# Moving the sampled tokens' state space steps of a hybrid decoder layer, and gating them apart

## The chip, the core and the metric

The kernel runs on one core of a Trainium2 chip. Five engines work side by side, each through its own instructions in order: TensorE (PE, with its weight loads PEld) multiplies matrices from on-chip memory into accumulator banks, VectorE (DVE) and ScalarE (ACT) compute on tiles of 128 partitions and empty those banks, GpSimd (POOL) computes on tiles, and SyncE (SP) issues nearly all DMA transfers. The metric is the device time of one execution in microseconds.

## The reference

One layer of a recurrent decoder for two groups of requests: one prompt of 1024 new tokens with empty states, and 8 sampled tokens, each with its own saved states. In the kernel the two lie side by side as 1032 columns.

```
h = rmsnorm(x);  q, f, i, g, z, xbc, dt = split(h @ w_in)
group A: 8 heads of a gated linear recurrence on q, f, i, own rmsnorm, times silu(g)
group B: xs, B, C = silu(conv4(xbc));  per head of 64 (16 heads, 2 groups of B and C):
         S = exp(A dt) S + dt x B^T ;  y = S C + D x
         y = rmsnorm over each half of y * silu(z)     (512 values a token)
x = x + concat(oA, y) @ w_out;  then a gated MLP with conv3, and a last rmsnorm
```

For the prompt group B is computed as a scan over chunks of 128 tokens. For a sampled token it is one step: scale the saved state (64 x 128 a head) by exp(A dt), add the outer product of dt x and B, store it as an output, multiply by C and sum. The change is about this step, "the step" below. The other outputs are the new states of both recurrences and of both convolutions.

## The kernel before, in words

*Projection jobs.* w_in is worked off in jobs of 128 output columns: x0 to x11 (convolution inputs of group B; x8 to x11 are B and C), z0 to z7, and f, q, v, sg for each of the 8 heads of group A. A job has three chunks of 344 tokens, each 24 matmuls (`in_job`, L290): 8 slices of the inner dimension, three products of split numbers (hh, hl are the high and low part of the normalised input, wh and wl of the weights). After each chunk `evict` empties the bank; `begin` runs at the job's start, and `load_ahead` (L217) has then just written the weight load of the job after it. The order of the jobs is x0 to x3, x9, x11, x4 to x7, z0 to z3, f0, q0, v0, sg0, z4 to z7, f1, q1, v1, sg1, then f, q, v, sg of heads 2 to 7.

*What runs beside them.* `drive` (L266) mixes a stream of other work into the jobs: it yields weights, and so many job matmuls are placed between its pieces. The first scan, `ssd(0)`, is mixed into the jobs from x9 to x7, the second, `ssd(1)`, into z0 to v0; sg0 and z4 to z7 run alone; head 0 of group A is mixed into f1 to sg1, head 1 into f2 to sg2, and so on. A scan's chunk is `ssd_front` (L530: csb is the decay matrix, xdt the scaled input, bg and xp transposes) and `ssd_back` (L563: yo from the state S, st the new state, yd the part within the chunk, sT at the end the state to be stored).

*Ticks.* Each call of `step` (L249) is a tick and one job matmul; a job and its end are 73 ticks. `after(n, work)` (L229) has a piece of work written n ticks later.

*Who sets the order.* Only TensorE's instructions run in the order in which they are written. Those of the other engines and of SyncE's queue are ordered by a planner when the kernel is built: it goes through the program with a model of the times and gives each engine what is ready and was written first. Once built, the order of each is fixed, and an instruction that waits holds up those behind it. `fetch` (L172) ties a load to the queue place of the weight load written last before it: it stands behind that one on SyncE, not ahead.

*Buffers.* Tiles are named by tags with a fixed number of buffers: "ld" has 2 (the states Sd of the step and Sh of the heads, 128 x 512), "d" has 4 (Bb and Cb of the step, vb of the heads), "z" has 4 (sz, the gate). Of accumulator banks the tag "nx" has one, for small products; `vd` at a head's start (L847), `od`, `odp` and `dms` in it, `ms` of the gate and others use it in turn.

*The step.* `ssm_decode(g, i)` (L628) does tile i (two heads of 64) of group g for the 8 tokens in two halves of 4: load B and C of the tokens to all partitions (Bb, Cb) and the state (Sd); scale Sd on ScalarE (L641, four activations); Bb times dt x on VectorE (L642); add (L643); store (L644); Sd times C on GpSimd (L645); sum on VectorE (L646). At the end L647 writes y into the last 8 columns of the tile Xg[g][i] (named xbc in the profile), beside the prompt's 1024. The four tiles of group 0 are written at the begin of x5, x7, z0 and z1, those of group 1 at the begin of z4 to z7.

*The gate.* A z job's `evict` (L672) multiplies Y, the tile with prompt and sampled columns, by silu(z) and collects the squares in gacc; `rstd` (L686) sums them over partitions with TensorE (ms), `rows` and `tail` (L703) scale the tile and store all 1032 columns into mix_d, from which the output projection reads.

Of the kernel before, what the change touches and what calls it, by code (L numbers as in the profile page):

```python
# [8 lines left out]
F32 = mybir.dt.float32  # L9
F32R = mybir.dt.float32r  # L10
U8 = mybir.dt.uint8
AF = mybir.ActivationFunctionType
ALU = mybir.AluOpType
# [3 lines left out]
P = 128  # L17
DM = 1024
T = 1024
ND = 8  # L20
NT = T + ND
CH = 344
NCH = 3
# [16 lines left out]
QW = NT // 4  # L40
# [10 lines left out]
def hybrid_layer(  # L51
# [9 lines left out]
    V, A, G, PE, SP = nc.vector, nc.scalar, nc.gpsimd, nc.tensor, nc.sync  # L61
# [5 lines left out]
    dram = ctx.enter_context(tc.tile_pool(name="dscr", bufs=1, space=DRAM))  # L67
# [3 lines left out]
    def nm(s):  # L71
        cnt[0] += 1
        return f"{s}_{cnt[0]}"
# [4 lines left out]
    const = part.enter_context(tc.tile_pool(name="const", bufs=1, side="right"))  # L78
    small = part.enter_context(tc.tile_pool(name="small", bufs=2, side="right"))
    tmp = part.enter_context(tc.tile_pool(name="tmp", bufs=1, side="right"))  # L80

    def tl(tag, name, dt=F32):
        w, n = TAGS[tag]
        return (work if tag in ("hT", "big", "e", "g") else tmp).tile([P, w], dt, tag=tag, bufs=n, name=nm(name))
# [4 lines left out]
    def bank(s, tag="mx"):  # L89
        return psmx.tile([P, 512], F32, tag=tag, bufs=NBANK[tag], name=nm(s))  # L90

    def mm(out, lhsT, rhs, start=True, stop=True):
        PE.matmul(out, lhsT, rhs, start=start, stop=stop)  # L93
# [55 lines left out]
    def col(name, i=0):  # L149
        c = vlay[name] + i  # L150
        return vcol[:, c:c + 1]
# [20 lines left out]
    def fetch(dst, src):  # L172

        with tc.issue_after(last_w[0].ins):
            SP.dma_start(dst, src)
# [53 lines left out]
    def after(n, work):  # L229

        later.append([n, work])
# [106 lines left out]
    Xg = [[None] * 4 for _ in range(2)]  # L338
    BT, CT, S = [None, None], [None, None], [None, None]
    last11 = const.tile([P, XT, 11], F32, name="last11")  # L340
    mix_d = dram.tile([16, P, NT], F32, name="mix_d")
# [13 lines left out]
    def xbc_evict(j, ext, c, cs, ps):  # L355
        e = min(cs.stop, T)
        A.copy(ext[:, 3 + cs.start:3 + e], ps[:, :e - cs.start])
        if c == 2:
            V.tensor_copy(ext[:, 3 + T:3 + T + 32].rearrange("p (b r) -> p b r", r=4)[:, :, 3:4],
                          ps[:, T - cs.start:].unsqueeze(2))  # L360
            V.tensor_copy(last11[:, j, :], ps[:, CH - 11:])

    def xbc_close(j, ext):
        G.tensor_copy(ext[:, 3 + T:3 + T + 32].rearrange("p (b r) -> p b r", r=4)[:, :, 0:3],
                      bufT[:, j, :].rearrange("p (b r) -> p b r", r=3))
        n = T + 32
        acc = tl("big", "xbc")
        conv_tail(acc, ext, 4, "cw", "cb", j, XT, n)
        A.activation(acc[:, :T], acc[:, :T], AF.Silu)
        A.activation(acc[:, T:NT], acc[:, T + 3:T + 32:4], AF.Silu)  # L370
        return acc

    def xbc_job(j, put):
        ext = []
        def begin():
            ext.append(xbc_open())
            if j in (5, 7):
                ssm_decode(0, (5, 7).index(j))

        in_job(f"x{j}", OFF_X + j * P, lambda c, cs, ps: xbc_evict(j, ext[0], c, cs, ps), begin=begin, end=lambda: put(xbc_close(j, ext[0])))  # L380

# [20 lines left out]
    ones = keep.tile([P, P], F32, name="ones")  # L402
# [24 lines left out]
    for c, cs in enumerate(chunks):  # L427
        ps = psmm.tile([P, 512], F32, tag="mm", name=nm("dt"))
# [9 lines left out]
    for i in range(9):  # L438
        n = P if i < 8 else ND
# [7 lines left out]
    d_bc = const.tile([P, 8], F32, name="d_bc")  # L447
# [61 lines left out]
    ddb = const.tile([P, 2, 8, ND], F32, name="ddb")  # L509
# [104 lines left out]
    def d4(t):  # L614
        return t.rearrange("p (b n) -> p b n", n=P)
# [12 lines left out]
    def ssm_decode(g, i):  # L628
        j = g * 4 + i
        xdd = small.tile([P, 2, ND], F32, tag="xdd", name=nm("xdd"))  # L630
        xdec = Xg[g][i][:, T:NT]
        V.tensor_tensor(xdd[:, 0, :], xdec, ddb[:, 0, j, :], op=ALU.mult)
        for b0 in (0, 4):
            bs = slice(b0, b0 + 4)
            Bb, Cb = tl("d", "Bb")[:, :512], tl("d", "Cb")[:, :512]
            for t_, r in ((Bb, 2 * g), (Cb, 2 * g + 1)):
                fetch(t_, bc_d[r, bs].rearrange("b n -> (b n)").unsqueeze(0).to_broadcast([P, 512]))
            Sd = tl("ld", "Sd")
            fetch(d4(Sd), state_ssm[0, bs, 2 * j:2 * j + 2].rearrange("b h p n -> (h p) b n"))
            for b in range(4):  # L640
                A.activation(d4(Sd)[:, b, :], d4(Sd)[:, b, :], AF.Copy, scale=ddb[:, 1, j, b0 + b:b0 + b + 1])  # L641
            V.tensor_tensor(d4(Bb), d4(Bb), cb(xdd[:, 0, bs]), op=ALU.mult)  # L642
            V.tensor_tensor(Sd, Sd, Bb, op=ALU.add)  # L643
            SP.dma_start(ssm_sample[0, bs, 2 * j:2 * j + 2].rearrange("b h p n -> (h p) b n"), d4(Sd))  # L644
            G.tensor_tensor(Cb, Sd, Cb, op=ALU.mult)  # L645
            V.tensor_reduce(xdd[:, 1, bs], d4(Cb), axis=mybir.AxisListType.X, op=ALU.add)  # L646
        V.scalar_tensor_tensor(xdec, xdec, d_bc[:, j:j + 1], xdd[:, 1, :], op0=ALU.mult, op1=ALU.add)  # L647

    def rstd_of(dst, tmp, ps, n):

        A.activation(dst, ps, AF.Abs_reciprocal_sqrt, bias=epsc, scale=1.0 / n)
        V.scalar_tensor_tensor(tmp, ps, n * EPS, dst, op0=ALU.add, op1=ALU.mult)
        V.scalar_tensor_tensor(tmp, tmp, -0.5 / n, dst, op0=ALU.mult, op1=ALU.mult)
        V.scalar_tensor_tensor(dst, tmp, 1.5, dst, op0=ALU.add, op1=ALU.mult)

    gr_d = dram.tile([2, 4, QW], F32, name="gr_d")

    def ssm_gate(g):
        acc = []

        def z_job(i):
            j = g * 4 + i

            def begin():
                if i == 0:
                    acc.append(tl("g", "gacc"))
                if g:
                    ssm_decode(1, i)
                elif i < 2:
                    ssm_decode(0, i + 2)  # L670

            def evict(c, cs, ps):  # L672
                Y = Xg[g][i][:, cs]
                sz = tl("z", "sz")[:, :CH]
                A.activation(sz, ps, AF.Silu)
                V.tensor_tensor(Y, Y, sz, op=ALU.mult)
                if i == 0:
                    A.activation(acc[0][:, cs], Y, AF.Square)
                else:
                    A.activation(sz, Y, AF.Square)  # L680
                    (V if g or i == 3 else G).tensor_tensor(acc[0][:, cs], acc[0][:, cs], sz, op=ALU.add)
                if i == 3 and c == NCH - 1:
                    after(36, rstd)
            in_job(f"z{j}", OFF_Z + j * P, evict, begin=begin)

        def rstd():  # L686
            ps = bank("ms", "nx")
            for q in range(4):
                mm(ps[32 * q:32 * q + 32, :QW], ones[:, 0:32], acc[0][:, q * QW:(q + 1) * QW])
            nt = tl("z", "nt")  # L690
            rstd_of(nt[:, :QW], tl("z", "nt")[:, :QW], ps[:, :QW], 512)
            SP.dma_start(gr_d[g], nt[::32, :QW])
            after(36, rows)

        def rows():
            fetch(acc[0][:, :NT], gr_d[g].rearrange("a t -> (a t)").unsqueeze(0).to_broadcast([P, NT]))
            after(20, lambda: spread(tail(), 6))

        def tail():
            for i in range(4):  # L700
                j = g * 4 + i
                Y = Xg[g][i][:, :NT]
                V.scalar_tensor_tensor(Y, Y, col("sn", j), acc[0][:, :NT], op0=ALU.mult, op1=ALU.mult)  # L703
                SP.dma_start(mix_d[8 + j], Y)
                yield

        for i in range(4):
            z_job(i)
# [110 lines left out]
    def head_in(h):  # L819
        t = {}  # L820

        def f_end():
            f, k = t["f"], tl("big" if h else "e", "k")
            A.activation(f[:, :NT], f[:, :NT], AF.Identity, bias=lbt2[:, 0, h:h + 1], scale=lbt2[:, 1, h:h + 1])
            V.tensor_scalar(k[:, :NT], f[:, :NT], -1.0, 1.0, op0=ALU.mult, op1=ALU.add)
            t["k"] = k

        for n, off, func in (("f", OFF_F, AF.Tanh), ("q", OFF_Q, AF.Silu), ("v", OFF_I, AF.Copy),
                             ("sg", OFF_G, AF.Silu)):
            def evict(c, cs, ps, n=n, func=func):  # L830
                A.activation(t[n][:, cs], ps, func, scale=0.5 if n == "f" else 1.0)

            def begin(n=n):
                t[n] = tl("e" if h == 0 and n == "f" else "big", n)

            if h == H - 1 and n == "sg":
                in_job_last(f"{n}{h}", off + h * P, evict, begin)
            else:
                in_job(f"{n}{h}", off + h * P, evict, begin, f_end if n == "f" else None)
        return t  # L840
# [539 lines left out]
    with tc.manual_schedule(engines={mybir.EngineType.PE}):  # L1380
# [56 lines left out]
        for r0 in range(0, FT - RND, RND):  # L1437
# [3 lines left out]
            for m in range(0, KT, 2):  # L1441
                wh, wl = wload(w_down[0, rows, m * P:(m + 2) * P], nk, 2 * P)
                for i in range(2):
# [3 lines left out]
                    for c, cs in enumerate(quarters):  # L1447
                        ps = down(lambda k: (wh[:, k, :], wl[:, k, :]), nk, slice(i * P, (i + 1) * P), acts, c)
# [14 lines left out]
    for c in (3, 0, 1, 2):  # L1463
        cs = quarters[c]
# [3 lines left out]
        for t0 in range(cs.start, cs.stop, P):  # L1468
            n = min(P, cs.stop - t0)
# [49 lines left out]
```

## Time and profile before

| | |
|---|---|
| median of 3 runs | 1765.24 us (1763.6 to 1767.99) |
| the profiled execution | 1764.89 us |
| its span, first to last instruction | 1763.2 us |
| TensorE busy | 1709.8 us, 97% |
| VectorE busy | 1097.8 us, 62% |
| ScalarE busy | 778.7 us, 44% |
| GpSimd busy | 478.8 us, 27% |
| mean granted TensorE clock | 0.995 |

The profile is of one execution. A row of the timeline gives start, length, engine, line of the kernel, operation, output and inputs, and in brackets the idle time of the engine just before, with what ended it. L93 is the helper that writes every matmul, so matmuls are told apart by their tiles. "mm" is a projection job. The granted clock is the share of full speed at which TensorE was allowed to run in a slice. A row of a group of instructions ends with count, busy time, mean length in ns, and the idle time before them with what ended it.

Where the parts lie in the span: the first scan from 107 to 213 us, the second to about 334, z4 to z7 from 343 to 389, the heads of group A from there to 890.

### The profile page before, as it was taken

What the parts mean: (1) busy time and instruction counts of PE and PEld (TensorE: products, weight loads), DVE (VectorE), ACT (ScalarE), POOL (GpSimd) and SP (SyncE); (2) the same over time, 40 slices, a digit from 0 to 9 for tenths busy, and PEclk for the clock granted to TensorE, in tenths of its full rate; (3) what the DMA queues carried; (4) which work ended last, traced back from release to release, by engine and by line L of the source; (5) the groups of instructions that cost most, each with busy time, mean ns of one, the idle gap of its engine ahead of it and who ended that gap; (6) DMA issues with size and microseconds to landing.
All of it is one profiled execution on the core that took longest, in us unless ns stands there. A gap on an engine that the chain in (4) does not pass through costs nothing. (4 is left out here: it accounts for less than half of the span.)

```text
span 1763.2 us, 38543 instructions
## 1 busy us (share of the span) xinstructions
PE 1709.8 (97%) x16115; PEld 1659.4 (94%) x16115; DVE 1097.8 (62%) x1978; ACT 778.7 (44%) x1422; POOL 478.8 (27%) x485
## 2 busy tenths in 40 slices
PE   7999899999999999999799999999999999999998
PEld 6998789899999999999799989999999999999997
DVE  6668966566554554566636687776667767445545
ACT  7577686444434344344423374343333434111114
POOL 2103231111110110111220355666666664000002
PEclk9999999999999999999999999999999999999999
DMA  5355644553232332234336832222222226422312
GB/s 166 65 148 149 173 120 143 167 169 120 83 93 57 98 87 72 77 110 144 114 115 210 250 123 73 73 85 82 88 73 73 79 82 214 153 83 78 98 61 97
DMA packets 250132, 200.23 MB, mean 114 GB/s; under 512 B 47252, under 2 KB 220870, under 8 KB 249942
## 3 DMA queue, kind: packets, MB, share of 16 engines
q1 hardware_dynamic: 249670, 197.68, 37.0%
q8 instruction: 126, 2.06, 0.5%
q14 instruction: 48, 0.39, 0.1%
q0 software_dynamic: 288, 0.10, 0.0%
HBM read 155.17 MB, written 46.95 MB: 115 GB/s over the span
## 5 line engine op out<-in xcount | busy, mean ns | idle before, releaser
L93 PE MATMUL mm<-hl,wh 128*128 128x344 f32 x1248 | 406.1, 326 | 0.0
L93 PE MATMUL mm<-hh,wh 128*128 128x344 f32 x1248 | 405.6, 326 | 0.0
L93 PE MATMUL mm<-hh,wl 128*128 128x344 f32 x1248 | 402.8, 323 | 0.8 <-issue 0.8
L93 PEld LDWEIGHTS mm<-hl,wh 128*128 128x128 f32 x1248 | 236.1, 189 | 4.8 <-issue 4.2
L93 PEld LDWEIGHTS mm<-hh,wh 128*128 128x128 f32 x1248 | 236.1, 189 | 4.2 <-issue 3.4
L93 PEld LDWEIGHTS mm<-hh,wl 128*128 128x128 f32 x1248 | 236.3, 189 | 1.4 <-issue 1.2
L190 ACT CAST wh<-ws 128x1024 fp32r<-128x1024 f32 x96 | 100.6, 1048 | 254.9 <-PE dn L93 134.9
L93 PE MATMUL ub<-uh,wh 128*128 128x258 f32 x704 | 199.5, 283 | 4.2 <-DVE fext L1332 2.7
L93 PE MATMUL ub<-uh,wl 128*128 128x258 f32 x704 | 198.7, 282 | 0.0
L93 PE MATMUL ub<-ul,wh 128*128 128x258 f32 x704 | 198.6, 282 | 0.0
L93 PE MATMUL dn<-ah,wh 128*128 128x256 f32 (+1 forms) x640 | 181.1, 283 | 2.0 <-DVE x L1449 2.0
L93 PE MATMUL dn<-al,wh 128*128 128x256 f32 (+1 forms) x640 | 180.6, 282 | 0.0
L93 PE MATMUL dn<-ah,wl 128*128 128x256 f32 (+1 forms) x640 | 180.1, 281 | 0.0
L192 DVE TENSOR_TENSOR wl<-ws,wh 128x1024 fp32r<-128x1024 f32 x88 | 108.8, 1236 | 78.5 <-ACT wh L190 77.7
L93 PE MATMUL ua<-uh,wh 128*128 128x258 f32 x528 | 149.3, 283 | 1.5 <-DVE val L1344 1.3
L93 PE MATMUL mm<-mh,wh 128*128 128x258 f32 x512 | 146.9, 287 | 3.0 <-ACT x L1077 1.8
L93 PE MATMUL ua<-ul,wh 128*128 128x258 f32 x528 | 149.1, 282 | 0.0
L93 PE MATMUL ua<-uh,wl 128*128 128x258 f32 x528 | 148.4, 281 | 0.0
L93 PE MATMUL mm<-ml,wh 128*128 128x258 f32 x512 | 145.4, 284 | 0.9 <-DVE ml L1037 0.9
L93 PE MATMUL mm<-mh,wl 128*128 128x258 f32 x512 | 145.2, 284 | 0.0
L93 PEld LDWEIGHTS ub<-uh,wh 128*128 128x128 f32 x704 | 133.0, 189 | 4.9 <-DVE fext L1332 2.9
L1282 DVE TENSOR_TENSOR wl<-wt,wh 128x512 fp32r<-128x512 f32 x88 | 89.1, 1031 | 73.8 <-ACT wh L1281 73.8
(353 smaller groups left out, 3981.9 us busy)
## 6 DMA issues: line engine op xcount, KB each, us to landing
ws<-in_w_in_dram SPq DMA_DIRECT2D x52, 512.0 KB
ws<-in_w_up_dram SPq DMA_DIRECT2D x44, 512.0 KB
ws<-in_w_out_dram SPq DMA_DIRECT2D x24, 512.0 KB
act_d<-val SPq DMA_DIRECT2D x22, 516.0 KB
al<-act_d SPq DMA_DIRECT2D x22, 516.0 KB
ws<-in_w_down_dram SPq DMA_DIRECT2D x22, 512.0 KB
ml<-mix_d SPq DMA_DIRECT2D x48, 172.0 KB
csb<-cs_d SPq DMA_DIRECT2D x32, 256.0 KB
```

Source lines behind the costliest of these rows:

```text
L93: PE.matmul(out, lhsT, rhs, start=start, stop=stop)
L190: A.copy(wh[:, :n], ws[:, :n])
L192: V.tensor_tensor(wl[:, :n], ws[:, :n], wh[:, :n].bitcast(F32), op=ALU.subtract)
L1282: V.tensor_tensor(lo[:, cs], sums[name], hi[:, cs].bitcast(F32), op=ALU.subtract)
```

## The change

The sampled columns of group B leave the tiles of the prompt. Their input goes into a small tile xdk (8 tiles x 8 tokens), their silu(z) into szd; the scan's tiles keep 1024 columns, and the prompt's gate works on these alone.

The step is taken apart. At its place it writes only dt x and the six loads (the state now ahead of B and C); 36 ticks later the first half up to the product with C, at 56 the second half, at 64 and 84 the sums. It is written elsewhere: group 0 at the begin of sg0, z4, z5 and z6, group 1 at the begin of v2, v3, v4 and v5.

The gate of the sampled columns is new: after the fourth tile of a group, 20 ticks later the product with szd, its squares and their sum over the tiles (`decode_gate`); 40 ticks later a matmul with ones into a bank "dgs" of tag "nx", the reciprocal root, the scaling, and one store of 4 x 128 x 8 values into mix_d (`decode_norm`).

```diff
+    xdk = const.tile([P, 8, ND], F32, name="xdk")
+    szd = const.tile([P, 8, ND], F32, name="szd")
...
-        A.activation(acc[:, T:NT], acc[:, T + 3:T + 32:4], AF.Silu)
+        A.activation(xdk[:, j, :] if j < 8 else acc[:, T:NT], acc[:, T + 3:T + 32:4], AF.Silu)
...
             ext.append(xbc_open())
-            if j in (5, 7):
-                ssm_decode(0, (5, 7).index(j))
...
-        xdec = Xg[g][i][:, T:NT]
+        xdec = xdk[:, j, :]
         V.tensor_tensor(xdd[:, 0, :], xdec, ddb[:, 0, j, :], op=ALU.mult)
+        got = []
         for b0 in (0, 4):
             bs = slice(b0, b0 + 4)
             Bb, Cb = tl("d", "Bb")[:, :512], tl("d", "Cb")[:, :512]
+            Sd = tl("ld", "Sd")
+            fetch(d4(Sd), state_ssm[0, bs, 2 * j:2 * j + 2].rearrange("b h p n -> (h p) b n"))
             for t_, r in ((Bb, 2 * g), (Cb, 2 * g + 1)):
                 fetch(t_, bc_d[r, bs].rearrange("b n -> (b n)").unsqueeze(0).to_broadcast([P, 512]))
-            Sd = tl("ld", "Sd")
-            fetch(d4(Sd), state_ssm[0, bs, 2 * j:2 * j + 2].rearrange("b h p n -> (h p) b n"))
+            got.append((bs, Bb, Cb, Sd))
+
+        def front(bs, Bb, Cb, Sd):
             for b in range(4):
...
             G.tensor_tensor(Cb, Sd, Cb, op=ALU.mult)
+
+        def back(bs, Bb, Cb, Sd):
             V.tensor_reduce(xdd[:, 1, bs], d4(Cb), axis=mybir.AxisListType.X, op=ALU.add)
-        V.scalar_tensor_tensor(xdec, xdec, d_bc[:, j:j + 1], xdd[:, 1, :], op0=ALU.mult, op1=ALU.add)
+        def end():
+            back(*got[1])
+            V.scalar_tensor_tensor(xdec, xdec, d_bc[:, j:j + 1], xdd[:, 1, :], op0=ALU.mult, op1=ALU.add)
+            if i == 3:
+                after(20, lambda: decode_gate(g))
+        after(36, lambda: front(*got[0]))
+        after(56, lambda: front(*got[1]))
+        after(64, lambda: back(*got[0]))
+        after(84, end)
+    def decode_gate(g):
+        js = slice(4 * g, 4 * g + 4)
+        dg = small.tile([P, 6, ND], F32, tag="dg", bufs=1, name=nm("dg"))
+        V.tensor_tensor(xdk[:, js, :], xdk[:, js, :], szd[:, js, :], op=ALU.mult)
+        V.tensor_tensor(dg[:, 0:4, :], xdk[:, js, :], xdk[:, js, :], op=ALU.mult)
+        V.tensor_reduce(dg[:, 4, :], dg[:, 0:4, :].rearrange("p j b -> p b j"), axis=mybir.AxisListType.X, op=ALU.add)
+        after(40, lambda: decode_norm(g, js, dg))
+    def decode_norm(g, js, dg):
+        ps = bank("dgs", "nx")
+        mm(ps[:, :ND], ones, dg[:, 4, :])
+        rstd_of(dg[:, 4, :], dg[:, 5, :], ps[:, :ND], 512)
+        for j in range(js.start, js.stop):
+            V.scalar_tensor_tensor(xdk[:, j, :], xdk[:, j, :], col("sn", j), dg[:, 4, :], op0=ALU.mult, op1=ALU.mult)
+        SP.dma_start(mix_d[8 + js.start:8 + js.stop, :, T:NT].rearrange("j p b -> p j b"), xdk[:, js, :])
...
-                if g:
-                    ssm_decode(1, i)
-                elif i < 2:
-                    ssm_decode(0, i + 2)
+                if g and i < 3:
+                    ssm_decode(0, i + 1)
...
+                if c == NCH - 1:
+                    G.tensor_copy(szd[:, j, :], sz[:, n:])
+                sz = sz[:, :n]
                 V.tensor_tensor(Y, Y, sz, op=ALU.mult)
...
-                V.scalar_tensor_tensor(Y, Y, col("sn", j), acc[0][:, :NT], op0=ALU.mult, op1=ALU.mult)
-                SP.dma_start(mix_d[8 + j], Y)
+                V.scalar_tensor_tensor(Y, Y, col("sn", j), acc[0][:, :T], op0=ALU.mult, op1=ALU.mult)
+                SP.dma_start(mix_d[8 + j][:, :T], Y)
...
             def begin(n=n):
+                if h == 0 and n == "sg":
+                    ssm_decode(0, 0)
+                elif 2 <= h <= 5 and n == "v":
+                    ssm_decode(1, h - 2)
```

More of the change, by code (lines that the diff above doesn't have):

```diff
@@ L635, in ssm_decode @@
             Bb, Cb = tl("d", "Bb")[:, :512], tl("d", "Cb")[:, :512]
+            Sd = tl("ld", "Sd")
+            fetch(d4(Sd), state_ssm[0, bs, 2 * j:2 * j + 2].rearrange("b h p n -> (h p) b n"))
             for t_, r in ((Bb, 2 * g), (Cb, 2 * g + 1)):
                 fetch(t_, bc_d[r, bs].rearrange("b n -> (b n)").unsqueeze(0).to_broadcast([P, 512]))
-            Sd = tl("ld", "Sd")
-            fetch(d4(Sd), state_ssm[0, bs, 2 * j:2 * j + 2].rearrange("b h p n -> (h p) b n"))
+            got.append((bs, Bb, Cb, Sd))
+        def front(bs, Bb, Cb, Sd):
             for b in range(4):
-                A.activation(d4(Sd)[:, b, :], d4(Sd)[:, b, :], AF.Copy, scale=ddb[:, 1, j, b0 + b:b0 + b + 1])
+                A.activation(d4(Sd)[:, b, :], d4(Sd)[:, b, :], AF.Copy, scale=ddb[:, 1, j, bs.start + b:bs.start + b + 1])
             V.tensor_tensor(d4(Bb), d4(Bb), cb(xdd[:, 0, bs]), op=ALU.mult)
@@ L654, in rstd_of @@
         V.scalar_tensor_tensor(dst, tmp, 1.5, dst, op0=ALU.add, op1=ALU.mult)
-    gr_d = dram.tile([2, 4, QW], F32, name="gr_d")
+    gr_d = dram.tile([2, 4, 256], F32, name="gr_d")
     def ssm_gate(g):
@@ L666, in begin @@
                     acc.append(tl("g", "gacc"))
-                if g:
-                    ssm_decode(1, i)
-                elif i < 2:
-                    ssm_decode(0, i + 2)
+                if g and i < 3:
+                    ssm_decode(0, i + 1)
             def evict(c, cs, ps):
+                cs = slice(cs.start, min(cs.stop, T))
+                n = cs.stop - cs.start
                 Y = Xg[g][i][:, cs]
@@ L688, in rstd @@
             for q in range(4):
-                mm(ps[32 * q:32 * q + 32, :QW], ones[:, 0:32], acc[0][:, q * QW:(q + 1) * QW])
+                mm(ps[32 * q:32 * q + 32, :256], ones[:, 0:32], acc[0][:, q * 256:(q + 1) * 256])
             nt = tl("z", "nt")
-            rstd_of(nt[:, :QW], tl("z", "nt")[:, :QW], ps[:, :QW], 512)
-            SP.dma_start(gr_d[g], nt[::32, :QW])
+            rstd_of(nt[:, :256], tl("z", "nt")[:, :256], ps[:, :256], 512)
+            SP.dma_start(gr_d[g], nt[::32, :256])
             after(36, rows)
         def rows():
-            fetch(acc[0][:, :NT], gr_d[g].rearrange("a t -> (a t)").unsqueeze(0).to_broadcast([P, NT]))
+            fetch(acc[0][:, :T], gr_d[g].rearrange("a t -> (a t)").unsqueeze(0).to_broadcast([P, T]))
             after(20, lambda: spread(tail(), 6))
@@ L701, in tail @@
                 j = g * 4 + i
-                Y = Xg[g][i][:, :NT]
-                V.scalar_tensor_tensor(Y, Y, col("sn", j), acc[0][:, :NT], op0=ALU.mult, op1=ALU.mult)
-                SP.dma_start(mix_d[8 + j], Y)
+                Y = Xg[g][i][:, :T]
+                V.scalar_tensor_tensor(Y, Y, col("sn", j), acc[0][:, :T], op0=ALU.mult, op1=ALU.mult)
+                SP.dma_start(mix_d[8 + j][:, :T], Y)
                 yield
```

## Prediction

> **What bounds the kernel now.** I read the page's first part, then a table of busy time by stage, the gaps of the TensorE timeline, and what the other engines waited for just ahead of each gap.
>
> ```profile
> PE 1709.8 (97%) x16115; PEld 1659.4 (94%) x16115; DVE 1097.8 (62%) x1978; ACT 778.7 (44%) x1422; POOL 478.8 (27%) x485
> ```
> ```profile
> 100.00:165.00 65.00, 65.00 (x451) 61.10 (x451) 53.38 (x76) 54.03 (x105) 15.31 (x20) 1.00 0.57 148
> 165.00:240.00 75.00, 66.93 (x439) 60.38 (x439) 61.02 (x103) 53.89 (x118) 21.11 (x18) 0.95 0.67 173
> ...
> 318.00:340.00 22.00, 19.12 (x119) 17.65 (x118) 15.82 (x28) 7.79 (x17) 3.67 (x3) 0.92 0.57 171
> 340.00:820.00 480.00, 477.69 (x6028) 460.84 (x6027) 256.96 (x483) 209.78 (x366) 44.73 (x34) 1.00 0.34 101
> ```
>
> TensorE is the bound: 1709.8 of 1763.2 us busy, in an order written by hand. A change that adds no matmuls worth naming can only move its idle time and its clock. The table (time, PE, PEld, DVE, ACT, POOL, granted clock, DMA share) shows where the change could reach: 165 to 240 us, the end of the first scan, loses 8.1 us and has a clock of 0.95; 318 to 340, the end of the second, loses 2.9 us at 0.92; 340 to 820, in which z4 to z7 and the heads run, loses 2.3 us in 480. The gaps one by one (start of the matmul, its length, in brackets the idle time before it and what ended it):
>
> ```profile
> 173.15 1.09 PE L93 MATMUL yd<-csb,xdt 128*64 128x128 f32 x16 [1.49 <-DVE xdt L557]
> 179.61 0.65 PE L555 MATMUL xp<-ident,xbc 128*128 128x128 f32 x4 [1.19 <-DVE ecs L577]
> 192.08 0.33 PE L548 MATMUL bg<-ident,xbc 128*128 128x128 f32 x1 [1.28 <-DVE S L583]
> 206.57 1.19 PE L93 MATMUL yo<-xbc,S 128*128 128x128 f32 x8 [2.00 <-DVE S L583]
> 227.64 0.33 PE L555 MATMUL xp<-ident,xbc 128*128 128x128 f32 x1 [1.96 <-ACT xbc L369]
> ...
> 329.83 0.66 PE L608 MATMUL sT<-ident,S 128*128 128x128 f32 x4 [2.54 <-DVE S L583]
> ```
> ```profile
> 170.00:180.00 10.00, 7.31 (x56) 6.11 (x55) 8.03 (x11) 7.67 (x19) 2.49 (x2) 1.00 0.62 167
> ...
> 200.00:210.00 10.00, 8.00 (x44) 6.24 (x46) 10.00 (x14) 5.78 (x15) 4.03 (x3) 0.88 0.43 98
> 210.00:220.00 10.00, 10.00 (x72) 9.77 (x69) 9.79 (x20) 4.51 (x10) 1.29 (x1) 0.95 0.72 185
> 220.00:230.00 10.00, 8.04 (x48) 7.78 (x47) 5.32 (x9) 9.24 (x18) 2.03 (x2) 0.90 0.90 222
> 230.00:240.00 10.00, 10.00 (x62) 9.22 (x62) 6.76 (x12) 9.94 (x23) 3.66 (x4) 0.93 0.37 105
> ...
> 330.00:340.00 10.00, 10.00 (x56) 10.00 (x56) 7.08 (x13) 4.60 (x9) 2.63 (x2) 0.83 0.50 140
> ```
>
> The gaps of 1.96 us and more are each followed by a spell of lower clock; those of 1.19 to 1.49 are not (1.00 from 170 to 180). A spell costs the clock missing in its slices: 10 x (0.12 + 0.05) = 1.7 us after 206.57, 10 x (0.10 + 0.07) = 1.7 after 227.64, 10 x 0.17 = 1.7 after 329.83. What VectorE did ahead of the gaps:
>
> ```profile
> 171.80 0.69 DVE L642 TENSOR_TENSOR Bb<-Bb,xdd 128x512 f32<-128x512 f32 x1 [2.83 <-DMA Bb<-bc_d]
> ...
> 188.03 0.69 DVE L646 TENSOR_REDUCE xdd<-Cb 128x4 f32<-128x512 f32 x1 [1.19 <-POOL Cb L645]
> 190.28 0.69 DVE L646 TENSOR_REDUCE xdd<-Cb 128x4 f32<-128x512 f32 x1 [1.56 <-POOL Cb L645]
> ...
> 326.25 0.69 DVE L642 TENSOR_TENSOR Bb<-Bb,xdd 128x512 f32<-128x512 f32 x1 [2.15 <-DMA Bb<-bc_d]
> 328.49 0.69 DVE L642 TENSOR_TENSOR Bb<-Bb,xdd 128x512 f32<-128x512 f32 x1 [0.94 <-DMA Bb<-bc_d]
> ```
>
> These are lines of the sampled tokens' step, and VectorE, which works in order, stands still in them with the scan's xdt and S queued behind. So the step is what stops the scan's matmuls at 173, 192 and 330 directly. The gaps at 180 and 207 follow while VectorE is full (10.00 of 10 from 200 to 210).
>
> **The change, part by part.** *The step leaves the first scan.* Four steps now run beside x4 to z1. Each is, by these rows, 8 x 0.39 = 3.1 us of ScalarE, 2 x (0.69 + 0.71 + 0.68) = 4.2 of VectorE, 2 x 1.34 = 2.7 of GpSimd, and on SyncE's queue six loads and two stores of 256 KB:
>
> ```profile
> L641 ACT ACTIVATE Sd<-Sd,ddb 128x128 f32<-128x128 f32 x64 | 20.5, 391 | 13.3 <-DMA Sd<-in_state_ssm_dram 13.2
> ...
> L645 POOL TENSOR_TENSOR Cb<-Sd,Cb 128x512 f32<-128x512 f32 x16 | 21.4, 1336 | 68.1 <-DVE Sd L643 57.9 <-DMA Sd<-in_state_ssm_dram 10.2
> L643 DVE TENSOR_TENSOR Sd<-Sd,Bb 128x512 f32<-128x512 f32 x16 | 11.3, 711 | 0.0
> L642 DVE TENSOR_TENSOR Bb<-Bb,xdd 128x512 f32<-128x512 f32 x16 | 11.0, 694 | 18.0 <-DMA Bb<-bc_d 18.0
> L646 DVE TENSOR_REDUCE xdd<-Cb 128x4 f32<-128x512 f32 x16 | 10.9, 683 | 14.3 <-POOL Cb L645 14.3
> ```
>
> With it go the waits above. I take all five gaps from 173 to 228 as gone: 1.49 + 1.19 + 1.28 + 2.00 + 1.96 = 7.9 us, and their two spells of low clock, 3.4. Ends: 11.3 us, and 1.49 + 1.28 = 2.8 if only the gaps go whose releaser stood directly behind a wait of the step. I take the first, because the stage before it (100 to 165) does the same convolutions and scan, with one step in it, without a single TensorE gap.
>
> *Where the first group's steps go.* They are written at the begin of sg0, z4, z5 and z6, with the work 36 ticks or more later. But what is written late is not run late:
>
> ```profile
> 347.22 0.44 ACT L675 ACTIVATE sz<-mm 128x344 f32<-128x344 f32 x1
> ```
> ```profile
> 298.41 0.38 SPq L189 DMA_DIRECT2D ws<-in_w_in_dram  x1
> ...
> 320.88 0.39 SPq L189 DMA_DIRECT2D ws<-in_w_in_dram  x1
> 321.31 0.58 SPq L175 DMA_DIRECT2D Bb<-bc_d  x1
> ```
>
> The step now written at z4 had its first VectorE work at 326.25, 21 us ahead of z4's first eviction, because its loads stand right behind the weight load of z5 (320.88) and the planner fills a free place with what its model has ready. After the change z4's step is that of the first group's second tile, behind the same weight load: the gap of 2.54 us at 329.83 and its 1.7 I leave as they are. sg0's step stands behind the weight load before, that of z4 (298.41), so it falls into 299 to 318, inside the second scan, which had no step there. Its price: 0 by the step written at x5, which cost no gap, up to 2.54 + 1.7 = 4.2 by the one at 326. Five steps fell into scans (four of them with gaps), for 11.3 + 4.2 = 15.5 us: 3.1 each, and I take that, +3.1. The steps of z5 and z6 replace those that ran there without a gap, with no scan beside them: 0, which z matmuls cover, and up to 4.2 each by the same row.
>
> *The second group beside v2 to v5.* The step moves behind the head's Sh tiles, which hold both "ld" buffers until the od matmuls, half-way through each head. There the stage's VectorE is busy 257 of 480 us and ScalarE 210 of 480, so 4.2 and 3.1 us a head are covered. Queued behind a late step are the next head's Sh loads and what VectorE does on them:
>
> ```profile
>   DMA Sh<-in_state_hgrn_dram: 16.7, 11
> ```
> ```profile
> 327.81 1.28 ACT L641 ACTIVATE Sd<-Sd,ddb 128x128 f32<-128x128 f32 x4 [7.35 <-DMA Sd<-in_state_ssm_dram]
> ```
>
> VectorE already waits for Sh 11 times, 1.5 us each, and the stage hides it: I take 0. Upper end: a wait of 7.35, less the 1.5 that is hidden, plus 1.7 of clock, 7.6 a head. The weight loads behind these loads on SyncE have room: the one at 320.88 is for z5, whose matmuls begin after z4's eviction at 347.
>
> *The gate of the sampled columns.* Eight copies on GpSimd and, for each group, two products, a reduction, three steps of the reciprocal root and four scalings of at most 128x32 on VectorE, some 2 us a group at 0.17 to 0.2 each; on ScalarE one 128x8 activation and up to two table loads; one small store. All of it lies beside matmuls of the stage above, cost 0 there. What is on TensorE's path: the new matmul "dgs" comes 20 + 40 + 84 = 144 ticks after the begin of z6 (and of v5), and a job and its end take 73 ticks. So it stands one matmul ahead of the end of z7 (and of sg5), and the next thing TensorE does is the transpose "vd" of head 0 (of head 5), into the same one-buffer bank "nx". It must wait until dgs has been read by ScalarE and VectorE. The nearest rows are the same operations on "dms":
>
> ```profile
> 440.33 0.29 PE L93 MATMUL dms<-od,ones 128*128 128x8 f32 x2
> ```
> ```profile
> 441.15 1.28 ACT L651 ACT_TABLE_LOAD   x1
> 442.45 0.27 ACT L651 ACTIVATE od<-dms,epsc 128x8 f32<-128x8 f32 x1
> ```
> ```profile
> 442.75 0.17 DVE L652 SCALAR_TENSOR_TENSOR od<-dms,od 128x8 f32<-128x8 f32 x1 [0.83 <-ACT od L651]
> ```
>
> With the table there: 0.27 + 0.17 after the matmul and some hand-over, less the last job matmul (65.0 / 451 = 0.14), so about 0.6 each, 1.2 in all; with the table load in the chain 442.92 - 440.33 = 2.6 plus 1.7 of clock, 4.3 each. I take the lower, as ScalarE has little to do between evictions at a job's end and a table load waits for no matmul. Here the next activation starts 0.02 us after the load's end. The Trainium skill ("ScalarE: Activation LUTs", What ACT_TABLE_LOAD costs) counts about 1.38 us of draining on top of the 1.28; the trace shows none of it, and by that rule the higher end would be 1.4 more each. The two dgs matmuls themselves: 2 x 0.29 = 0.6. The prompt's gate shrinks from 1032 to 1024 columns: nothing.
>
> *Sum:* -7.9 - 3.4 + 3.1 + 1.2 + 0.6 = -6.4 us against the profiled execution's 1764.9 (span 1763.2 and 1.7 around it), which gives 1758.5. The median of the runs, 1765.2, is 0.3 above it: 1758.8.
>
> **Rivals.**
> *A. All gaps of the scans go:* the staged step lands later in VectorE's order, and sg0's and z4's cost nothing, the gap at 330 included: -11.3 - 4.2 + 1.8 = -13.7, 1751. For: at sg0 and z4 no scan stands next to where the steps are written. Against: the 21 us of advance.
> *B. The step was not what limited the scan.* VectorE was busy 61 of 75 us there; the gaps at 180, 207 and 228 name ecs, S and ScalarE's Silu, none of them the step's. If they stay with their clock, -2.8 + 3.1 + 1.8 = +2.1, 1767. Against: the calm stage from 100 to 165.
> *C. Slower: Sh behind Sd.* In heads 1 to 4 VectorE is planned to take the next head's Sh when the model has it, but its load now waits for the step's store to release "ld". From a wait of 1.5 + 2.0 = 3.5 us on, a head loses 2.0 of TensorE and 1.7 of clock: 4 x 3.7 = 14.8, and -6.4 + 14.8 = +8.4, 1773.6. For: the 7.35 above. Against: no gap of note between 340 and 820 in spite of 16.7 us of such waits.
> *D. The clock does not come back with the gaps.* Then 3.4 stay, and a step in a scan costs (7.9 + 2.5) / 5 = 2.1: -7.9 + 2.1 + 1.8 = -4.0, 1761.2. Against: each gap of 1.96 to 2.54 us has its spell and no shorter one has. The Trainium skill ("TensorE: Matmul & The Clock Gate", Part 1: The HAM clock gate) lets the throttle return only after an idle window of about 3.4 us, which would speak for D; in this trace shorter gaps did it, so the row decides.
>
> **How the numbers follow.** The forecast 0.47 (its own range 1753 to 1763), A 0.13, B 0.19, C 0.16, D 0.05. A measurement of this kernel can tell about 0.3%, 5.3 us, from no change: below 1759.9 is faster, above 1770.5 slower. Faster: 0.30 of the forecast and A, 0.43. Slower: 0.15 of C and 0.04 of B, 0.19. The rest, 0.38, is the same. The range runs from A (1750) to 1771, which leaves out most of C.
>
> **What would show it.** Right: no VectorE wait for Bb or Cb between 165 and 240, no TensorE gap over 1 us there and a clock of 1.00; L642 still well ahead of z4, and a gap near the sT transposes; a TensorE wait at vd in heads 0 and 5 alone, near 0.6 us; no gaps in the second halves of heads 1 to 4. Wrong: gaps that keep their place in the first scan with no step near (B); waits for Sh over 3.5 us (C); new stalls of the scan between 299 and 318 above 4 us.

## The result, and the profile after

The changed kernel takes 1775.53 us in the median of 7 runs (1770.23 to 1781.17), the kernel before 1763.96 beside it (1760.81 to 1767.99): a ratio of 1.0068, with an interval of 1.0051 to 1.0086. It is slower by 12 us, where 6 us less were forecast. The profiled execution of it took 1778.31 us, with a span of 1776.5; it is 2.8 us above the median, so the prices read from its trace may add up to that much more than the medians show.

The table by stage of the changed kernel (time, TensorE, its weight loads, VectorE, ScalarE, GpSimd, granted clock, DMA share, GB/s):

```profile
165.00:240.00 75.00, 75.00 (x531) 69.40 (x532) 52.09 (x87) 56.43 (x108) 16.74 (x18) 1.00 0.34 94
305.00:328.00 23.00, 18.86 (x117) 17.41 (x116) 21.08 (x35) 10.01 (x25) 6.57 (x5) 0.93 0.71 193
380.00:390.00 10.00, 10.00 (x77) 9.16 (x81) 5.17 (x17) 4.66 (x7) 4.33 (x4) 0.83 0.41 107
440.00:720.00 280.00, 266.25 (x3472) 254.88 (x3470) 148.52 (x297) 119.13 (x214) 33.31 (x25) 0.97 0.37 109
```

The end of the first scan, which had 66.93 busy us of 75 and a clock of 0.95, is full at 1.00. The stage of the heads, in which TensorE stood idle for only 0.8 us before, is not. The same 280 us of the kernel before:

```profile
440.00:720.00 280.00, 279.16 (x3788) 267.69 (x3788) 143.36 (x276) 120.57 (x195) 26.02 (x20) 1.00 0.29 84
```

The changed kernel's gaps of over 1 us in TensorE's timeline, from the end of the second scan to head 5:

```profile
318.29 0.63 PE L609 MATMUL sT<-ident,S 128*128 128x128 f32 x4 [3.51 <-DVE S L584]
379.97 0.27 PE L886 MATMUL vd<-ident,v 128*8 128x128 f32 x1 [2.54 <-DVE dg L684]
467.14 0.75 PE L93 MATMUL a<-q,f 128*32 128x32 f32 x64 [2.33 <-DVE q L925]
535.50 0.75 PE L93 MATMUL a<-q,f 128*32 128x32 f32 x64 [2.81 <-DVE q L925]
601.85 0.75 PE L93 MATMUL a<-q,f 128*32 128x32 f32 x64 [2.15 <-DVE q L925]
667.20 0.97 PE L93 MATMUL a<-q,f 128*32 128x32 f32 x64 [1.39 <-DVE q L925]
711.69 0.36 PE L886 MATMUL vd<-ident,v 128*8 128x128 f32 x1 [2.54 <-DVE dg L684]
```

Four of the seven stand in the first halves of heads 1 to 4, where the prediction saw nothing, and where the code writes nothing of the step. To see what each place costs with its clock, I took from the traces, one execution of each kernel, the start of each projection job and subtracted. The table gives this for some jobs, in us against the kernel before; a step from one column to the next is what the stretch between them cost. The other rows are of the first experiments below, whose jobs are the same.

| kernel | x4 | v0 | z7 | v1 | v2 | v3 | v4 | v5 | q6 | sg7 |
|---|---|---|---|---|---|---|---|---|---|---|
| changed | -0.3 | -12.8 | -11.6 | -7.5 | -2.8 | +2.2 | +7.7 | +10.6 | +14.1 | +14.0 |
| loads tied | -1.1 | -13.6 | -12.3 | -8.3 | -8.2 | -8.1 | -8.1 | -7.9 | -5.0 | -5.1 |
| another bank for dgs | -0.4 | -12.9 | -12.2 | -12.9 | -8.9 | -4.1 | -1.4 | +2.8 | +3.8 | +3.7 |
| store on GpSimd's queue | -1.1 | -13.6 | -12.4 | -9.6 | -9.7 | -9.7 | -9.7 | -9.7 | -7.8 | -7.8 |
| tied, with the bank | -0.6 | -13.1 | -11.7 | -13.1 | -13.2 | -12.4 | -12.4 | -11.5 | -11.8 | -11.9 |

So the first scan gains 12.5 (x4 to v0) and the second's end loses 1.2 (v0 to z7); the gate at head 0 costs 4.1 (z7 to v1) and at head 5 3.5 (v5 to q6); between them four heads cost 4.7, 5.0, 5.5 and 2.9, 18.1 in all (v1 to v5). That makes +14.0 at sg7. The span's end is 13.3 later.

What VectorE does ahead of the gap at 467, in head 1 (L647 is the product of B, L642 in the kernel before and L649 where the loads are tied):

```profile
456.29 1.27 DVE L647 TENSOR_TENSOR Bb<-Bb,xdd 128x512 f32<-128x512 f32 x1 [1.61 <-DMA Bb<-bc_d]
464.18 0.69 DVE L647 TENSOR_TENSOR Bb<-Bb,xdd 128x512 f32<-128x512 f32 x1 [6.62 <-DMA Bb<-bc_d]
...
466.32 0.67 DVE L925 TENSOR_TENSOR q<-q,tt 128x512 f32<-128x512 f32 x1
```

VectorE stands for 6.62 us in the second product of a step whose place in the code, v2, begins at 480.1. Behind it are the products that make q, for which TensorE waits at 467.14. Why the load is late is read from SyncE's queue and GpSimd, and then from the waits of SyncE's queue (instruction, what it waited for, us in total, times, longest):

```profile
449.05 0.38 SPq L1062 DMA_DIRECT2D mix_d<-sg  x1
449.48 0.43 SPq L175 DMA_DIRECT2D Bb<-bc_d  x1
456.04 3.08 SPq L907 DMA_DIRECT2D out_dram<-Sh  x2
459.17 0.90 SPq L175 DMA_DIRECT2D Cb<-bc_d  x1
460.16 0.40 SPq L175 DMA_DIRECT2D Bb<-bc_d  x1
```
```profile
454.74 1.28 POOL L906 TENSOR_TENSOR Sh<-Sh,vb 128x512 f32<-128x512 f32 x1
455.97 1.04 POOL L904 TENSOR_TENSOR vb<-vb,k 128x512 f32<-128x512 f32 x1
457.09 1.61 POOL L906 TENSOR_TENSOR Sh<-Sh,vb 128x512 f32<-128x512 f32 x1
```
```profile
SPq L907 <- POOL Sh L906: 61.3, 16, 6.5
```

Between the two loads of B the planner has put the two stores of the head's state Sh. They wait for GpSimd's sums, the second of which ends at 458.70 (457.09 + 1.61), and the second load of B is issued only at 460.16. It needs GpSimd as well, but only the first sum: of the four "d" buffers two hold the head's vb and two the step's first Bb and Cb, and the first vb is done with when that sum ends, at 456.02 (454.74 + 1.28; the run with the store on another queue, below, shows this load leave at just that point). The other 4.1 us it stands behind the second store and a load of C.

### The profile page after: what moved, and what is told of

It reads as the page before. It is cut to its first block, busy times and chain, and to the rows that moved or that the text cites. A ratio compares the mean times of both kernels' runs of the same rounds, so it can differ in the third digit from the quotient of the medians.

```text
span 1776.5 us, 38604 instructions
## 1 busy us (share of the span) xinstructions
PE 1717.3 (97%) x16119; PEld 1667.5 (94%) x16119; DVE 1094.4 (62%) x1998; ACT 782.2 (44%) x1428; POOL 482.4 (27%) x493
```

## The experiments

Two theories on the heads. *Early product:* the planner takes the next step's loads of B and C, which need only a free "d" buffer, and the product behind them into the first half of the head, and VectorE waits there for a load that SyncE's queue holds up behind the head's stores. *Rival C of the prediction:* the next head's Sh is late behind the step's Sd in the "ld" buffers.

**Loads tied.** B and C are issued only after their own state's load, which waits for "ld" until half-way through the head.

```diff
-            fetch(d4(Sd), state_ssm[...])
+            with tc.issue_after(last_w[0].ins):
+                sl = SP.dma_start(d4(Sd), state_ssm[...])
...
-                fetch(t_, bc_d[r, bs]...)
+                with tc.issue_after(sl.ins):
+                    SP.dma_start(t_, bc_d[r, bs]...)
```

> The changed kernel with one edit: each half's loads of B and C are tied behind the load of its state on SyncE's queue, so in heads 1 to 4 they come only when the od matmuls have freed the state's buffer. Theory 'early product' (the Bb product of the second group stands in the first half of a head, on VectorE's queue ahead of the head's own work, while its load is late): the gaps of 2.33, 2.81, 2.15 and 1.39 us and the low clock behind them go, 18 us over the four heads, 1757 us. Theory C of the prediction (Sh behind Sd): nothing changes, 1775 us.

Measured 1760.18 us, ratio 0.9984 (0.9969 to 1.0): 15.4 below the changed kernel by the medians, 18.3 by the profiled executions. The heads cost 0.4 in place of 18.1 (v1 to v5 in the table above), and the stage is full again:

```profile
440.00:720.00 280.00, 276.86 (x3826) 265.24 (x3825) 161.34 (x312) 127.74 (x228) 37.19 (x28) 1.00 0.39 113
```
```profile
479.07 0.69 DVE L649 TENSOR_TENSOR Bb<-Bb,xdd 128x512 f32<-128x512 f32 x1 [2.87 <-DMA Bb<-bc_d]
```

The product of head 1 now comes at 479, beside v2 where it is written. It still waits 2.87 us for its load, and TensorE doesn't notice, because nothing that it needs soon stands behind. The Sd and Sh loads share "ld" as before: rival C's mechanism is out.

**Store on GpSimd's queue.** VectorE's order at L647 stays; only the head's store leaves SyncE's queue.

```diff
-            SP.dma_start(hgrn_sample[0, bs, h]..., d4(Sd))
+            G.dma_start(hgrn_sample[0, bs, h]..., d4(Sd))
```

> The changed kernel with one edit: the store of the heads' sampled states (out_dram<-Sh) is issued from GpSimd's queue instead of SyncE's, so the second half's loads of B and C no longer stand behind a store that waits for GpSimd. VectorE's order stays. Theory 'loads held up in SyncE's queue': waits for Bb in heads 1 to 4 fall from 6.6 to under 3 us and most of the 18 us goes, 1758 to 1764 us. Rival 'the place in VectorE's order alone': gaps in the first halves stay, 1772 us or more.

Measured 1762.14 us, ratio 0.9986 (0.9974 to 0.9998). SyncE's queue, GpSimd and VectorE in head 1, and a row of the waits of SyncE's queue that the changed kernel doesn't have:

```profile
446.73 0.38 SPq L1062 DMA_DIRECT2D mix_d<-sg  x1
...
452.75 0.32 SPq L175 DMA_DIRECT2D Bb<-bc_d  x1
```
```profile
451.10 1.62 POOL L906 TENSOR_TENSOR Sh<-Sh,vb 128x512 f32<-128x512 f32 x1
```
```profile
454.11 0.68 DVE L647 TENSOR_TENSOR Bb<-Bb,xdd 128x512 f32<-128x512 f32 x1
455.82 0.96 DVE L647 TENSOR_TENSOR Bb<-Bb,xdd 128x512 f32<-128x512 f32 x1 [1.03 <-issue]
```
```profile
SPq L175 <- POOL Sh L906: 28.4, 10, 3.2
```

The second load of B is issued 0.03 us after GpSimd's first sum ends (451.10 + 1.62 = 452.72). That is 6.0 us after the store into mix_d, in the changed kernel 11.1 (460.16 - 449.05). The products are as early in VectorE's order as there (in head 1 they are its instructions 556 and 557 in both kernels), and the heads cost nothing (-9.6 to -9.7). So the early product does no harm by itself, nor does the load's own wait for GpSimd. It takes both, the early place and a load behind a store that waits, and taking away either one is enough. More "d" buffers were not tried.

**Unstaged.** The whole step is written at its begin, with none of the 36 to 84 ticks between its parts. The gate keeps its place.

```diff
-            if i == 3:
-                after(20, lambda: decode_gate(g))
-        after(36, lambda: front(*got[0]))
-        after(56, lambda: front(*got[1]))
-        after(64, lambda: back(*got[0]))
-        after(84, end)
+        front(*got[0])
+        back(*got[0])
+        front(*got[1])
+        end()
+        if i == 3:
+            after(104, lambda: decode_gate(g))
```

> The changed kernel with the stages of the step written at once at the step's begin (no 36, 56, 64 and 84 ticks; the gate of the sampled tokens stays where it was). Theory 'readiness sets the place': the Bb products stand at almost the same places of VectorE's queue, the time stays within 4 us of 1775.5. Rival 'the ticks hold the stages back': waits for loads grow, above 1780 us.

Measured 1778.53 us, ratio 1.0073 (1.0046 to 1.01): 3 us from the changed kernel, with the same gaps (2.13 at the same matmul of head 1, 2.54 at vd). In VectorE's order the first four products of B of group 0 are instructions 386, 400, 402 and 416, and 386, 399, 402 and 412 in the changed kernel; the eight of group 1 have the same places in both. The ticks hold back almost nothing: the planner had advanced the parts past them anyway.

**Another bank for dgs.** The small product of the gate goes into one of the four banks of the tag "mx" (the default of `bank`) and no longer shares the one "nx" bank with the transpose vd.

```diff
-        ps = bank("dgs", "nx")
+        ps = bank("dgs")
```

> The changed kernel with one edit: the matmul dgs of the sampled tokens' gate goes into one of the four 'mx' banks instead of the single 'nx' bank. Theory 'vd behind dgs': the two gaps of 2.54 us before vd and their low clock go, 4.5 us at head 0 and 3.6 at head 5, so 1767 us. Rival (vd would have waited for something else in its place): 1775 us.

Measured 1768.83 us, ratio 1.0023 (1.0012 to 1.0034), 6.7 below the changed kernel. Both gaps at vd are gone (z7 to v1 -0.7 in place of +4.1, v5 to q6 +1.0 in place of +3.5), and the clock at head 0 with them:

```profile
380.00:390.00 10.00, 10.00 (x188) 9.12 (x187) 8.77 (x23) 6.14 (x11) 5.94 (x5) 1.00 0.52 151
```

The heads still lose 15.7 (v1 to v5): the two losses are separate.

**Tied, with the bank.** Both edits.

> The two edits that each took away a part of the loss, together: the loads of B and C wait for their own state's load, and the matmul dgs has a bank of its own. If the two losses are separate, they add up: the changed kernel's 1775.5, less 18 for the four heads, less 8 for the two waits at vd, is 1749.5 (1747 to 1753), about 0.8% below the kernel before: no TensorE gap over 1 us in 440 to 665, none at vd in heads 0 and 5, the one of about 3.5 at sT still there. If one of them only stood in the other's place (the stall moves to the next tile of the head, or the weight load falls behind), 1756 to 1760.

Measured 1752.34 us (1751.42 to 1754.45), ratio 0.9926 (0.991 to 0.9941): below both kernels, and 23.2 below the changed one, of some 26 expected. The two losses add up. Of the seven gaps only the one at sT is left (3.69 us).

**Group 0 later.** With both edits, the first group's four steps one place later: all at z5, z6, z7 and v1, or only sg0's taken out of the second scan.

```diff
-                if g and i < 3:
-                    ssm_decode(0, i + 1)
+                if g and i:                    # all later
+                    ssm_decode(0, i - 1)
...
+                if g and i < 3:                # only sg0's
+                    ssm_decode(0, i)
...
-                if h == 0 and n == "sg":
-                    ssm_decode(0, 0)
+                if h == 1 and n == "v":        # in both
+                    ssm_decode(0, 3)
```

> The same two edits, and the first group's four steps written one place later: at z5, z6, z7 and the v of head 1 in place of sg0, z4, z5 and z6. Theory: the gap of 3.5 us at sT, the 0.6 at yo and the low clock after them (0.17 of 10 us) come from the steps of sg0 and z4, which fall into the second scan; one place later only one step is near it, and it is written a stage after the scan. Then 3.5 + 0.6 + 1.7 = 5.8 less than the run with the two edits alone, 1744 (1742 to 1747), and S at 317 comes without a wait for Bb ahead of it. Rival: the scan's last state is late by itself (VectorE's own work in 305 to 318), and the gap at sT stays at 2.5 or more: 1748 to 1752.

> The two edits, and only the step of sg0 is taken out of the second scan: the first group's four steps are written at z4, z5, z6 and the v of head 1. This leaves at the scan's end the one step that the kernel before had there. The prediction put the step of sg0 at 3.1 us, and the gap of 2.54 at sT with its 1.7 of clock on the step of z4. If that split holds, the gap at sT is 2.5 again, the 0.6 at yo is near 0.3, and the time is 1.2 to 3 us under the run with the two edits alone (1752.3): 1749.5 to 1751. If the step of sg0 alone makes the gap, it goes to under 1 us: 1747 to 1748. If ScalarE's evictions in z6 and z7 lose again what the scan gains (2.8 us in the run with all four steps later): 1752 to 1755.

All later: 1755.54 us, ratio 0.9942 (0.9925 to 0.9959), 3.2 above the two edits alone, where 5.8 less was expected. The theory on the scan held, and the time missed. The gap at sT is gone:

```profile
305.00:328.00 23.00, 21.90 (x148) 20.69 (x147) 13.14 (x24) 9.79 (x21) 2.52 (x3) 1.00 0.49 149
```

z5 starts 4.1 us earlier than with the two edits alone (-15.8 against -11.7). But z6 gives 2.8 of it back, 2.0 of them in three matmuls that wait for ScalarE to empty their bank. The longest wait, 1.30, is for an eviction behind the step's scaling and a cast of weights:

```profile
357.53 0.97 ACT L648 ACTIVATE Sd<-Sd,ddb 128x128 f32<-128x128 f32 x3
358.41 1.03 ACT L190 CAST wh<-ws 128x1024 fp32r<-128x1024 f32 x1
359.34 0.45 ACT L709 ACTIVATE sz<-mm 128x344 f32<-128x344 f32 x1
```
```profile
359.84 0.42 PE L93 MATMUL mm<-hh,wh 128*128 128x344 f32 x1 [1.30 <-ACT sz L709]
```

The rest goes by v1, where the two are level (-12.8 and -13.1): TensorE stops for 1.38 us at 394.48, and the profile names no cause (the last section has more of such stops). At sg7 they are still level (-11.7 and -11.9). The spans are 3.5 apart by what comes behind, which no run explains.

Only sg0's: 1756.12 us, ratio 0.9956 (0.9939 to 0.9973), 3.8 above the two edits alone. None of the times and gaps expected of the scan came; the loss that z6 and z7 were to bring (1752 to 1755) didn't come either (z5 to f1 0.0). The gap at sT is no smaller with one step less in the scan:

```profile
318.67 0.69 DVE L649 TENSOR_TENSOR Bb<-Bb,xdd 128x512 f32<-128x512 f32 x1 [3.33 <-DMA Bb<-bc_d]
...
322.13 0.68 DVE L584 TENSOR_TENSOR S<-S,st 128x512 f32<-128x512 f32 x1
```
```profile
322.95 1.09 PE L609 MATMUL sT<-ident,S 128*128 128x128 f32 x4 [4.43 <-DVE S L584]
```

The step written at z4 is alone there, its load of B is late (3.33 us), and S stands behind it: one step is enough for the whole gap. (Its profiled execution, 1762.36, was the longest of the six; 3.0 us of that arise before x0.)

**Store on GpSimd's queue, with the bank.**

> The head's store from GpSimd's queue in place of the tie, and the bank for dgs. If what costs is the load of B behind the store and nothing in VectorE's own order, this gives the same as the tie with the bank: 1775.5 - 19 - 8 = 1748.5 (1747 to 1753). If the order of VectorE costs too, 2 to 4 us more than the tie with the bank.

Measured 1760.9 us, ratio 0.9975 (0.9962 to 0.9989): 12 over what was expected, and 8.6 over the tie with the bank. The heads from v1 to v5 cost 0.1, so VectorE's order isn't it. By the two traces it is 5.6 behind the tie with the bank at v1, after a stop of TensorE for which the profile names no cause, then 3.6 at sg7, and loses 5.0 more behind it, where the granted clock is lower. These are the rows of this kernel, then of the tie with the bank:

```profile
398.00 0.25 PE L93 MATMUL a<-q,f 128*32 128x32 f32 x2 [3.40 <-issue]
...
820.00:860.00 40.00, 31.98 (x489) 30.24 (x487) 28.49 (x45) 18.09 (x42) 17.89 (x17) 0.79 0.46 143
```
```profile
820.00:860.00 40.00, 32.76 (x492) 31.14 (x480) 27.57 (x49) 16.99 (x40) 15.74 (x13) 0.87 0.49 149
```

Whether the stores on GpSimd's queue cause either is not settled. The other kernel with them has 0.79 in that window too, but no such stop at 398.

## Why the prediction was wrong, step by step

*The step leaves the first scan* (-11.3): right. No product of B falls between 165 and 240 us (the first is at 302.5), TensorE is full there at a clock of 1.00, and the stretch gained 12.5. All five gaps went, also those at which VectorE was merely full, and the two spells of low clock with them; rivals B and D fall. Rival A falls at the other scan, where the gap at sT stayed.

*Where the first group's steps go* (+3.1 for sg0, 0 for z5 and z6): the sign was right, the size 1.2, and the split was wrong. What VectorE had ahead of the last S of the scan:

```profile
313.19 0.68 DVE L647 TENSOR_TENSOR Bb<-Bb,xdd 128x512 f32<-128x512 f32 x1
313.79 0.67 DVE L653 TENSOR_REDUCE xdd<-Cb 128x4 f32<-128x512 f32 x1
314.38 0.68 DVE L648 TENSOR_TENSOR Sd<-Sd,Bb 128x512 f32<-128x512 f32 x1
315.60 1.35 DVE L647 TENSOR_TENSOR Bb<-Bb,xdd 128x512 f32<-128x512 f32 x1 [0.54 <-DMA Bb<-bc_d]
...
317.47 0.67 DVE L584 TENSOR_TENSOR S<-S,st 128x512 f32<-128x512 f32 x1
```

Parts of the step stand back to back ahead of S. The gap grew from 2.54 to 3.51; it goes when both steps leave the scan, and stays when sg0's alone does. So a share of sg0's own isn't shown. The steps at z5 and z6 cost nothing, as said (z4 to z7 stay at -11.6).

*The gate of the sampled columns* (0.6 at each vd, upper end 4.3): the wait and its place were right, the value was the wrong end. It came to 4.1 and 3.5. The reason given for the lower end, that a table load waits for no matmul, failed in ScalarE's order:

```profile
377.09 1.04 ACT L190 CAST wh<-ws 128x1024 fp32r<-128x1024 f32 x1 [2.09 <-PE mm L93]
378.16 1.28 ACT L683 ACT_TABLE_LOAD   x1
379.45 0.27 ACT L683 ACTIVATE dg<-dgs,epsc 128x8 f32<-128x8 f32 x1
```

The load itself waits for nothing, but ahead of it stands a cast of weights that waited 2.09 us for matmuls. So cast, table load and activation all lie in the chain from dgs to vd, and a spell of clock (0.83 from 380 to 390) follows. By the rule of the Trainium skill that was weighed there ("ScalarE: Activation LUTs", What ACT_TABLE_LOAD costs), 1.38 us of draining would come on top; the activation starts 0.01 us after the load's end, so the trace again shows none.

*The second group beside v2 to v5* (0): this is the step that failed, for +18.1 us. With all other terms as forecast, -6.4 + 18.1 = +11.7, and +13.3 was measured between the spans. The prediction looked at what would stand behind the step on SyncE's queue and in the "ld" buffers. It did not ask what would stand ahead of it, nor where VectorE would get its work. It had in its own text what it needed: the step of z4 ran 21 us ahead of its place because its loads were ready. The same advance put the steps of v2 to v5 a half head early (456.3 and 464.2 for a place at 480.1), where the stores of Sh wait for GpSimd on the same queue. The cost is gaps of 2.33 + 2.81 + 2.15 + 1.39 = 8.7 us, a smaller one of 0.45 or 0.67 behind each, 2.2 in all, and the clock. These are the stretches behind the four gaps:

```profile
469.00:473.00 4.00, 4.00 (x43) 3.97 (x33) 3.48 (x6) 2.71 (x4) 0.00 (x0) 0.57 0.49 135
537.00:542.00 5.00, 5.00 (x66) 4.97 (x52) 4.33 (x8) 3.11 (x6) 0.00 (x0) 0.66 0.23 61
602.00:610.00 8.00, 7.33 (x151) 7.18 (x144) 5.83 (x10) 5.16 (x10) 0.00 (x0) 0.57 0.25 68
667.00:677.00 10.00, 9.09 (x201) 8.36 (x201) 6.19 (x11) 7.39 (x14) 0.00 (x0) 1.00 0.20 56
```

The clock missing is 4 x 0.43 = 1.7, 5 x 0.34 = 1.7, 8 x 0.43 = 3.4 and nothing, 6.8 in all, and 8.7 + 2.2 + 6.8 = 17.7 of the 18.1. The rest of the sum nearly cancels: the two gates cost 7.6 in place of 1.8, and the two scans came out 3.1 better than forecast, so that -12.5 + 1.2 + 7.6 + 18.1 = +14.4 stands against -6.4.

*Rival C* had the sign, the four heads and nearly the time (1773.6), and the wrong mechanism, so that its time came near by chance. Sh is not late: VectorE's waits for it fell from 16.7 us in 11 to these:

```profile
  DMA Sh<-in_state_hgrn_dram: 11.0, 9
```

The gaps are in the first halves of the heads, not at Sh. What "would show it" named was enough to tell the two apart.

*The clock after a gap.* Of the seven gaps listed above, those of 2.15 us and more were each followed by a lower clock, and that of 1.39 by none, as the prediction had read it from the kernel before. The Trainium skill ("TensorE: Matmul & The Clock Gate", Part 1: The HAM clock gate), which asks for an idle window of about 3.4 us, again doesn't describe these rows. But the length of the gap alone doesn't decide either. With the loads tied, the gap of 2.54 at vd of head 5 (694.11) has no spell behind it:

```profile
690.00:700.00 10.00, 7.46 (x171) 6.97 (x169) 7.03 (x20) 5.30 (x7) 0.00 (x0) 1.00 0.61 185
```

Nor has one of 2.71 at 870.28 in the changed kernel (1.00 from 868 to 878), nor one of 2.72 at 1058.83 in the kernel before (1.00 from 1058 to 1064), outside the stretches that the prediction read. In the unstaged kernel a gap of 1.33 at 666.49, the same place as that of 1.39, has one (0.51 from 668 to 671).

## What to carry to other kernels

Where a planner like this one orders the queues, a piece of work runs where its inputs are ready, not where it is written: before moving it, ask for its earliest possible place, and price it there. On a queue that issues in order, a transfer that is ready is late if it stands behind a store that waits; either tie its issue to something that comes when it is wanted, or take the store off that queue. A small product put between long stages wants another bank than the next stage's first matmul, and its table load counts in full, as at head 0 here, if anything that waits stands ahead of it.

## What the runs showed that was not expected

A spell of low clock seems to come in pieces of one price, and how many follow a gap is open. By the rows above it cost 1.7 us after gaps of 2.33 and 2.81, and twice that, 3.4, after the shorter one of 2.15. In the window from 820 to 860 the mean clock was 0.91, 0.87 and 0.79 in three kernels (the tie, the tie with the bank, the store on GpSimd's queue with the bank); that is 3.6, 5.2 and 8.4 us, near two, three and five times 1.7.

TensorE can stop with nothing to wait for that the profile shows. At the last two matmuls of one group of 64 small ones, at the start of head 0's work, it stood 3.40 us in the last kernel above, 1.47 in the kernel before, and not at all in the tie with the bank. Of the ten kernels six stop at this very matmul, for 0.54 to 3.40 us, and two (group 0 later) two matmuls behind it, for 1.38 and 0.74:

```profile
407.04 0.22 PE L93 MATMUL a<-q,f 128*32 128x32 f32 x2 [1.47 <-issue]
```

I made no run to settle it.
